# Two-layer hybrid trunk on one core: mixers reworked, three buffers for RWKV's Gram matrices, one for its loaded projections

## Chip, cores and metric

One core of one Trainium2 chip runs the whole program in one launch. The metric is the device time of an execution in microseconds (us), lower is better. PE is the tensor engine (matrix products), DVE the vector engine, ACT the scalar engine, POOL the general-purpose engine, SP the engine whose queue issues most of the DMA transfers.

## What is computed

A trunk of two layers over 1024 prompt tokens and 32 sample tokens (8 sequences of 4), width 1024. Each layer projects its input, runs three groups of heads side by side, projects back, normalises, and runs a gated feed-forward part with a short convolution.

```python
for l in range(DEPTH):                                   # 2
    p = x @ w_in[l]                                      # 1024 -> 1440 | 976 | 1280 columns
    y_a, ... = _rwkv7_mix(p_rw, ...)                     # 6 heads, state 64x64 each
    y_b, ... = _gla_mix(p_gl, ...)                       # 5 heads, chunks of 64
    y_c, ... = _ret_mix(p_rt, ...)                       # 5 heads, rotary, fixed decay
    x = _layer_norm(ALPHA * x + concat([y_a, y_b, y_c]) @ w_out[l])
    f = conv_ffn(x)                                      # gelu(a) * b, 2816 wide, conv of 3 taps
    x = _layer_norm(ALPHA * x + f)

def step(s, inp):                                        # RWKV-7, per token
    r_t, w_t, a_t, b_t, k_t, v_t = inp
    sa = einsum('bhvk,bhk->bhv', s, a_t)
    s = s * w_t + sa[..., None] * b_t + v_t[..., None] * k_t
    return s, einsum('bhvk,bhk->bhv', s, r_t)

def _rms_heads(o):                                       # GLA and retention, per head
    return o * lax.rsqrt(jnp.mean(jnp.square(o), -1) + 1e-6)
```

Outputs are the two token streams and all new states.

## The kernel before

**Tiling.** Tokens are columns in three blocks of 384, 384 and 288 (the last holds the 32 samples first). Channels are rows in tiles of 128. The large products take each operand in two parts (a rounded high part and the rest, made by `split`, L186: ACT copies, POOL or DVE subtracts), and three products per tile and k (`mm3`, L251). The smaller products are plain fp32: each shows as two matmul instructions, a transpose as one.

**Order.** `Tensor` (L101) pins the order of PE's instructions to the order in which the program emits them, and keeps an estimated clock. Work is written as streams that yield either a wait in us, mostly out of the table `AFTER` (L36), or an event of another stream. `run` (L142) emits the first stream that is ready by the estimate, and a filler stream where none is. `post` (L133) puts off a DMA issue in the same way. So PE's order is fixed before the launch: if an operand comes later than the table says, PE stands there, and all behind it.

**Layer, in order.**

1. `group_a(0)` (L431): RWKV's twelve column tiles over block 0, one after the other (`gemm_steps`, L270). Weights come piece by piece through `Feed` (L203): four pieces of split weights at a time, two pieces to a column tile. In layer 0 the input itself is loaded and split here (L291); in layer 1 it comes channel tile by channel tile out of the LayerNorm of layer 0 (`normed`, L1474).
2. RWKV with filler (L909). Four streams over nine batches of 128 tokens (the ninth is the samples): `fronts` loads the projections (tile `x`, XB buffers) and makes the operands `ra` and `bk` (L473); `grams` makes the products within a chunk (`gps` in PSUM, masked by DVE into `gm`, GB buffers, L537) and starts the triangular solve; `toks` makes token-major operands (L563); `chains` joins the solution (`rwkv_merge`, L647) and runs the two chunks that carry the state (`rwkv_core`, L678). The solve (L621) goes to DRAM and back, spread over 96 partitions, with 62 dependent small DVE operations, then by DMA back into `gm`; its buffers `N` and `U` are single. Waits between batches: front i needs `tok` of i-1 and `chained` of i-3; gram i needs `chained` of i-GB, GB = 2; tok i needs `done` of i-2 (L793 to L815). PSUM for all of these is `pm`, two banks. The filler is `group_a` of blocks 1 and 2 and then `group_b` (L847), the token-major columns of GLA and retention (`gt`).
3. GLA, retention, the output projection and its LayerNorm (L1346): nine token tiles each through `gla_front`, `gla_back`, `ret_front`, `ret_back`; `finish` (L979) is the RMS norm and gate at the end of each of the 18. Its inverse root is `rsqrt` (L238): twelve DVE operations on [128, 5]. `yrows` transposes the rows back, `out_proj` (L1315) projects a block and sums for the LayerNorm; `stats` (L945) multiplies the sums with a matrix of ones (`lnm`, `lnv`), ACT takes Ln and Exp; `steps` (L959) applies it channel tile by channel tile: subtract (DVE), multiply (DVE), scale (ACT), split (ACT, POOL).
4. The feed-forward part (L1358 on): up-projection (`pu`), convolution on DVE, gate, down-projection (`pd`). Its first tiles use block 0, then 1, then 2 (`up_blocks`, L1426). PSUM: `pg` three banks, `pd` five.

Of the kernel before, what the change touches and what calls it, by code (L numbers as in the profile page):

```python
# [34 lines left out]
# expected times (us) from a step to what it makes ready  # L35
AFTER = {"key": 5.93, "sh": 3.5, "rkv": 2.0, "block": 6.0, "blockin": 2.5, "x": 3.0, "operands": 8.0, "gram": 0.9, "tv": 0.9, "tb": 0.9, "solve": 24.0, "ud": 4.5, "joined": 4.0, "mask": 1.5, "gd": 4.5, "x11": 1.28, "x21": 1.4, "x22": 0.6, "z": 1.4, "s": 1.58, "am": 2.0, "sx": 1.0, "sout": 3.0, "y": 7.3, "gate": 1.4, "state": 2.5, "done": 7.0, "turn": 2.5, "tokin": 3.36, "ev": 2.25, "gexp": 2.6, "gqt": 1.6, "rrot": 5.5, "rqt": 2.0, "at": 2.5, "qm": 0.8, "vx": 0.9, "gstate": 1.2, "tk": 4.5, "gateout": 4.0, "yin": 2.2, "yout": 4.5, "gnext": 1.2, "rout": 8, "rnext": 0.8, "yt": 0.5, "yready": 1.79, "ln": 3.0, "lnk": 1.5, "lns": 3.0, "ln1": 3.0, "ln2": 9.0}  # L36
# [18 lines left out]
# constant columns  # L55
# [10 lines left out]
class Event:  # L66
    """A time on the tensor engine from which something it has to wait for is expected."""
# [7 lines left out]
class Stream:  # L75
    """Work on the tensor engine in bursts: yields the time (us) until the next one can start, or an Event or a condition."""
# [24 lines left out]
class Tensor:  # L101
    """The tensor engine, its instructions kept in the order of the program, with an estimate of its time (us)."""

    def __init__(self, tc, engine):
        self.tc, self.engine, self.t, self.last, self.posts = tc, engine, 0.0, None, []
        Event.clock = self.clock
# [4 lines left out]
    def order(self, ins, cols, passes):  # L111
        ins = ins.ins
# [20 lines left out]
    def post(self, after, do):  # L133
        """Calls `do` when the time has come: a store that would hold up its queue before."""
# [7 lines left out]
    def run(self, streams, filler):  # L142
        """Emits the streams, the first ready one first, and the filler where none is; ends with the streams."""
# [14 lines left out]
def step_kernel(ctx: ExitStack, tc: tile.TileContext, xT, wA, wB, wO, wU, wD, pp, pb, lora, bg, bgk, shT, cvT, srw, sgl, srt,  # L158
# [27 lines left out]
    def split(dst_h, dst_l, src, le=None):  # L186
        """The two parts of src; returns the instructions."""
        return A.copy(dst_h, src), (le or G).tensor_tensor(dst_l, src, dst_h.bitcast(F32), ALU.subtract)  # L188
# [14 lines left out]
    class Feed:  # L203
        """Weights in two parts, piece after piece ([P, k, c] each), as far ahead as there is room."""
# [28 lines left out]
        def k(self, first, k):  # L233
            """The parts of row k of the matrix whose first piece is `first`, and whether its piece ends with it."""
# [3 lines left out]
    def rsqrt(pl, x, mul, add):  # L238
        """1 / sqrt(x * mul + add), by Newton's steps from the exponent's half."""
# [16 lines left out]
    def xtiles(what, n):  # L256
        """The two parts of a block; before the high part of the third one there is room for the low parts of its samples."""
# [4 lines left out]
    def gemm_ch(w, xs, n, name):  # L262
        """One M-tile of channel-major output over block n."""
        ps = pg.tile([P, 512], F32, tag="g", name=name)[:, :NB[n][1]]
# [1411 lines left out]
```

## Time and profile before

| | |
|---|---|
| device time, median of 3 runs | 3442.24 us (3440.7 to 3452.11) |
| span of the profiled execution | 3430.9 us |
| instructions in it | 59397 |
| PE / DVE / ACT / POOL busy | 3198.4 / 2068.6 / 1434.7 / 1332.6 us |
| layer 0: block 0's projection | 0 to 94 us, PE busy 84.87 |
| layer 0: end of `out_proj` to the first columns of `pu` | 921 to 945 us, PE busy 17.54 |
| layer 1: end of layer 0 to the end of block 0's projection | 1694 to 1840 us, PE busy 122.32 |
| layer 1: GLA, retention, output | 2285 to 2616 us, PE busy 288.35 |
| layer 1: its feed-forward part | 2640 to 3385 us, PE busy 743.88 |

The span is the profiler's, from the first to the last instruction of the program; the device time of the profiled execution itself is not given, and the median of the runs is 11.3 us above the span. A row of a table of groups gives line, engine, operation, names written and read, tile and shapes, count, busy time in us, mean ns of one, then idle time ahead of them and what ended it. A row of the timeline gives start, length, engine, line, names, count, and in brackets the engine's idle time ahead of it and what ended it. A row of the stages gives length, busy time of PE, of its weight loads (PEld), of DVE, ACT and POOL, the granted share of PE's clock, the DMA share and GB/s. Busy time of matrix products is stretched where the clock was granted by half.

### The profile page before, as it was taken

How to read it: one execution, taken by the hardware profiler on the slowest of the kernel's cores; microseconds unless marked ns; L12 is line 12 of the kernel's file. 1: busy time of each engine (PE TensorE's matmuls, PEld its weight loads, DVE VectorE, ACT ScalarE, POOL GpSimd, SP SyncE). 2: the span in 40 equal slices, each digit the busy share in tenths (PEclk: the TensorE clock that was granted, in tenths of full speed). 3: DMA queues.
4: the chain of work that ended last, by engine and by line, in shares of the span. 5: the costliest groups of instructions: out<-in, count | busy, mean ns of one | idle time of the engine just before them, and what ended most of it. 6: DMA issues, size and time to landing. Idle time of an engine off the chain costs nothing.

```text
span 3430.9 us, 59397 instructions
## 1 busy us (share of the span) xinstructions
PE 3198.4 (93%) x22110; PEld 2975.9 (87%) x22110; DVE 2068.6 (60%) x5037; ACT 1434.7 (42%) x3208; POOL 1332.6 (39%) x1660
## 2 busy tenths in 40 slices
PE   9889999988899999999888999999788999999995
PEld 8778888776799999999877888887777999999995
DVE  3577565776756544454746866646777564545457
ACT  6554332334543334333575543323346423333335
POOL 5443222224553334333565522221336433433345
PEclk9789999998999999999998999999989999999998
DMA  7333213433311111111154432234433111111111
GB/s 249 112 110 99 79 54 102 139 115 102 106 60 47 44 44 50 50 44 50 56 164 140 133 91 68 63 128 119 129 94 100 48 44 44 56 44 44 44 44 56
DMA packets 233261, 288.24 MB, mean 84 GB/s; under 512 B 65212, under 2 KB 146908, under 8 KB 232972
## 3 DMA queue, kind: packets, MB, share of 16 engines
q1 hardware_dynamic: 223852, 271.98, 26.3%
q10 hardware_dynamic: 9120, 12.47, 1.2%
q8 instruction: 173, 2.83, 0.4%
q14 instruction: 116, 0.95, 0.1%
HBM read 225.94 MB, written 58.43 MB: 83 GB/s over the span
## 4 chain that ended last, share of the span: by engine, by line
PE 70%; DVE 16%; DMA 4%; ACT 4%; issue 3%; POOL 2%; SPq 1%; ACTq 0%; DVEq 0%; POOLq 0%
PE pu L128 27%; PE pd L128 13%; PE gt L128 9%; PE pa L128 5%; PE po L128 3%; DVE tm L630 2%; DVE U L632 2%; PE zy L128 2%; PE gps L128 2%; PE rop L128 1%; DVE c L1401 1%; PE gop L128 1%; POOL wil L188 1%; DMA N<-gd 1%; DVE s L940 1%
## 5 line engine op out<-in xcount | busy, mean ns | idle before, releaser
L1401 DVE SCALAR_TENSOR_TENSOR c<-u,ppt,c 128x32 f32<-128x32 f32 (+1 forms) x704 | 395.8, 589 | 545.5 <-ACT c L1392 523.8
L188 POOL TENSOR_TENSOR wil<-wir,wih 128x512 fp32r<-128x512 f32 (+1 forms) x264 | 366.3, 1395 | 365.8 <-ACT wih L188 361.2
L128 PE MATMUL gt<-wih,xh 128*128 128x320 f32 (+1 forms) x1008 | 340.1, 339 | 0.9 <-DVE mx L388 0.9
L1448 DVE TENSOR_TENSOR acc<-acc,pd 128x384 f32<-128x384 f32 (+1 forms) x480 | 247.7, 518 | 139.5 <-PE pd L128 137.5
L128 PE MATMUL gt<-wil,xh 128*128 128x320 f32 (+1 forms) x1008 | 316.1, 315 | 6.5 <-POOL wil L188 5.2
L128 PE MATMUL gt<-wih,xl 128*128 128x320 f32 x896 | 281.6, 314 | 0.0
L188 ACT CAST wih<-wir 128x512 fp32r<-128x512 f32 (+1 forms) x296 | 185.6, 637 | 162.4 <-PE po L128 71.5
L128 PE MATMUL pa<-xh,wih 128*128 128x384 f32 (+1 forms) x576 | 216.5, 376 | 20.4 <-DVE mx L388 11.8
L630 DVE TENSOR_TENSOR tm<-U,N 96x60 f32<-96x60 f32 (+24 forms) x558 | 179.1, 321 | 69.9 <-DMA N<-gd 48.4
L128 PEld LDWEIGHTS gt<-wih,xh 128*128 128x128 f32 (+1 forms) x1008 | 187.5, 186 | 38.6 <-issue 21.9
L128 PE MATMUL pa<-xl,wih 128*128 128x384 f32 (+1 forms) x576 | 201.4, 350 | 3.3 <-POOL xl L188 3.0
L128 PE MATMUL pa<-xh,wil 128*128 128x384 f32 (+1 forms) x576 | 200.7, 348 | 3.6 <-POOL wil L188 2.2
L128 PEld LDWEIGHTS gt<-wil,xh 128*128 128x128 f32 (+1 forms) x1008 | 188.5, 187 | 10.2 <-POOL wil L188 9.1
L188 POOL TENSOR_TENSOR hl<-c,hh 128x384 fp32r<-128x384 f32 x132 | 128.1, 971 | 159.6 <-ACT hh L188 133.0
L632 DVE TENSOR_TENSOR U<-U,tm 96x60 f32<-96x60 f32 (+24 forms) x558 | 170.3, 305 | 14.0
L128 PEld LDWEIGHTS gt<-wih,xl 128*128 128x128 f32 x896 | 173.1, 193 | 0.0
L1392 ACT ACTIVATE c<-pu,ppt 128x384 f32<-128x384 f32 (+1 forms) x264 | 172.8, 655 | 0.0
L1380 ACT COPY u<-pu 128x384 f32<-128x384 f32 x176 | 84.1, 478 | 195.2 <-PE pu L128 195.1
L188 ACT CAST hh<-c 128x384 fp32r<-128x384 f32 x132 | 64.4, 488 | 222.4 <-DVE c L1407 222.3
L128 PEld LDWEIGHTS pa<-xh,wih 128*128 128x128 f32 x576 | 119.7, 208 | 35.1 <-DVE mx L388 13.2
L128 PE MATMUL po<-yh,wih 128*128 128x384 f32 (+1 forms) x384 | 138.9, 362 | 9.1 <-DVE ac L1325 6.7
L128 PE MATMUL po<-yh,wil 128*128 128x384 f32 (+1 forms) x384 | 131.7, 343 | 3.7 <-DVE wil L188 3.7
(810 smaller groups left out, 9862.6 us busy)
## 6 DMA issues: line engine op xcount, KB each, us to landing
wir<-in_wA_dram SPq DMA_DIRECT2D x144, 256.0 KB
wir<-in_wO_dram SPq DMA_DIRECT2D x96, 256.0 KB
wir<-in_wB_dram SPq DMA_DIRECT2D x56, 320.0 KB
tokd<-ev SPq DMA_DIRECT2D x112, 160.0 KB
x<-rkvd SPq DMA_DIRECT2D x16, 576.0 KB
tk<-tokd SPq DMA_DIRECT2D x16, 480.0 KB
rkvd<-mx SPq DMA_DIRECT2D x36, 192.0 KB
tk<-tokd SPq DMA_DIRECT2D x16, 400.0 KB
```

Of the source, the lines that this page charges most:

```text
L128: self.order(self.engine.matmul(out, lhsT, rhs, start=start, stop=stop), cols, 4 if rhs.dtype == F32 else 1)
L188: return A.copy(dst_h, src), (le or G).tensor_tensor(dst_l, src, dst_h.bitcast(F32), ALU.subtract)
L630: V.tensor_tensor(tm, U[:, 0:nr, i:i + 1].to_broadcast([4 * ns, nr, 31 - i]), N[:, i:i + 1, i + 1:32].to_broadcast([4 * ns, nr, 31 - i]), ...
L632: V.tensor_tensor(U[:, 0:nr, i + 1:32], U[:, 0:nr, i + 1:32], tm, ALU.add)
L940: self.ends["V"] = V.tensor_tensor(self.s1, acc[0] if k == 1 else self.s1, acc[k], ALU.add)
L1380: A.copy(u[:, 2:386], ps)
L1392: A.activation(c[:, :W], ps, AF.Identity, scale=pc(PP_CV + 4 * t + 2), bias=pc(PP_CV + 4 * t + 3))
L1401: V.scalar_tensor_tensor(cv, src, pc(PP_CV + 4 * t + tap), cv, ALU.mult, ALU.add)
L1448: V.tensor_tensor(acc[n][m], acc[n][m], ps, ALU.add)
```

## The change

- **Pairs of row halves.** Products over 64 rows are emitted alternately for rows 0 to 63 and 64 to 127, each half into its own PSUM bank: `zw`/`za` in `rwkv_front`, the two heads of a pair in `rwkv_gram` (now eight products at a time and one yield of 2 x 0.9 us where there were two of 0.9), and the heads of `ret_front`, whose k no longer carries zeros in the other head's rows (one copy of four columns in place of a copy and two scalings).
- **Transposes.** `tv` and the samples' `tb` in `rwkv_tok` use the transpose instruction, not a product with the identity.
- **Buffers.** GB from 2 to 3, XB from 2 to 1.
- **Table.** Grams of the first two batches wait 5.5 us longer; `x11` goes from 1.28 to 3.0 us.
- **Two column tiles at once.** The first two column tiles of `group_a(0)` run k by k together (`gemm_two`).
- **LayerNorm.** In `steps`, where parts are asked for, multiplication and the split's subtraction alternate between DVE and POOL by channel tile. The statistics' products of block 2 are held back (`Tensor.hold`) and put behind the first two `pu` tiles over block 0; those two take their banks from `pd`.
- **`finish`.** The inverse root is Ln and Exp on ACT, with the table set that has both named ahead of them, in place of `rsqrt`.

```diff
-AFTER = {..., "x11": 1.28, ...}
+AFTER = {..., "early": 5.5, ..., "x11": 3.0, ...}
-GB = 2
-BK, XB = 1, 2
+GB = 3
+BK, XB = 1, 1
...
+    def hold(self, do):
+        self.held = []
+        do()
+        held, self.held = self.held, None
+        return lambda: [self.order(*h) for h in held]
...
+    def gemm_two(feed, first, xs, n, names):
+        ps = [pg.tile([P, 512], F32, tag="g", name=name)[:, :NB[n][1]] for name in names]
+        xh, xl, _ = xs[n]
+        for k in range(KD):
+            for i, p in enumerate(ps):
+                h, lo, _ = feed.k(first + 2 * i, k)
+                mm3(p, h, lo, xh[:, k], xl[:, k], k == 0, k == KD - 1)
+            for _ in range({3: 1, 7: 3}.get(k, 0)):
+                feed.free()
+            if k < KD - 1:
+                yield 0
+        return ps
...
         def group_a(n):
-                ps = yield from gemm_steps(feed, 2 * (n * NA + q), xs, n, f"pa{m}_{n}", True)
+                if n == q == 0:
+                    two = yield from gemm_two(feed, 0, xs, n, [f"pa{i}_{n}" for i in MS[:2]])
+                if two:
+                    ps = two.pop(0)
+                else:
+                    ps = yield from gemm_steps(feed, 2 * (n * NA + q), xs, n, f"pa{m}_{n}", True)
...
         def rwkv_front(s):
-            for i, z in enumerate((zw, za)):
-                for j in range(NPAIR):
+            for j in range(NPAIR):
+                for i, z in enumerate((zw, za)):
...
-            yield AFTER["operands"]
+            yield AFTER["operands"] + (AFTER["early"] if s.b < 2 else 0)
...
         def rwkv_gram(s):
                 for j0, j1 in ((0, 2), (2, 3)):
+                    gps = [pmt("gps")... for _ in range(2)]
+                    for j in range(j0, j1):
+                        for c in range(2):
+                            for h in range(2):
+                                hs = slice(h * 64, h * 64 + 64)
+                                TE.matmul(gps[h][:, j - j0, c], bk(j, c)[hs], ra(j, c)[hs], start=True, stop=True)
                     for h in range(2):
-                        hs = slice(h * 64, h * 64 + 64)
-                        gps = pmt("gps")...
-                        for j in range(j0, j1):
-                            for c in range(2):
-                                TE.matmul(gps[:, j - j0, c], bk(j, c)[hs], ra(j, c)[hs], start=True, stop=True)
-                        V.tensor_tensor(g5[:, j0:j1, :, h], gps, ...)
-                        yield AFTER["gram"]
+                        V.tensor_tensor(g5[:, j0:j1, :, h], gps[h], ...)
+                    yield 2 * AFTER["gram"]
...
         def rwkv_tok(s):
-                TE.matmul(tv[:W, j * P:(j + 1) * P], s.v[:, j], ident, start=True, stop=True)
+                TE.transpose(tv[:W, j * P:(j + 1) * P], s.v[:, j], ident)
...
         class LayerNorm, steps:
-                    (V if hl or k % 2 else G).tensor_tensor(a, a, s2, ALU.mult)
+                    ((G if k % 2 else V) if hl else (V if k % 2 else G)).tensor_tensor(a, a, s2, ALU.mult)
...
-                        for ins, e in zip(split(hl[0][:, k], hl[1][:, k], a), "AG"):
+                        for ins, e in zip(split(hl[0][:, k], hl[1][:, k], a, V if k % 2 else G), "AV" if k % 2 else "AG"):
...
         def finish(op, rows, dst, gate, nw):
-            A.activation(sq, dst, AF.Square)
+            first = A.activation(sq, dst, AF.Square)
...
-            sm = rsqrt(gp_, sm, 1.0 / 64, 1e-6)
+            ins = TE.after(A.preload_act_table_set("natural_log_exp_and_others"), first)
+            TE.after(A.activation(sm, sm, AF.Ln, scale=1.0 / 64, bias=eps(1, rows)), ins)
+            A.activation(sm, sm, AF.Exp, scale=-0.5)
...
         def ret_front(s, tt):
-            A.copy(qT[:, 0:2], tp[:, 0:2 * rows].rearrange("p (g t) -> p g t", g=2))
-            for h in range(2):
-                A.activation(qT[:, 2 + h:6:2], tp[:, 2 * rows:4 * rows]..., AF.Copy, scale=C("h2")[:, h:h + 1])
+            A.copy(qT[:, 0:4], tp[:, 0:4 * rows].rearrange("p (g t) -> p g t", g=4))
...
+            sp = [front("rsp")[:rows, 0:(3 - i) * rows].rearrange("p (h t) -> p h t", t=rows) for i in range(2)]
             for h in range(4):
-                TE.matmul(sp[:rows, h * rows:(h + 1) * rows], qT[:, 2 + h], qT[:, h // 2], start=True, stop=True)
-            s4 = front("rs4")[:rows, 0:rows]
-            TE.matmul(s4, qT[:64, 7], qT[:64, 6], start=True, stop=True)
+                hs = slice((h % 2) * 64, (h % 2) * 64 + 64)
+                TE.matmul(sp[h % 2][:, h // 2], qT[hs, 2 + h // 2], qT[hs, h // 2], start=True, stop=True)
+            TE.matmul(sp[0][:, 2], qT[:64, 7], qT[:64, 6], start=True, stop=True)
...
         def out_proj(n):
-            yield AFTER["ln"]
-            ln.stats()
+            yield AFTER["ln"] if n < 2 else 0
+            if n < 2:
+                ln.stats()
+            else:
+                stats3.append(TE.hold(ln.stats))
...
         def up_conv(t, i, n, w, prev):
-            ps = gemm_ch(w, x1, n, f"pu{t}")
+            ps = gemm_ch(w, x1, n, f"pu{t}", None if t % NJ or n else pd.tile([P, 512], F32, tag="d", name="pu"))
...
         def up_blocks(j, between):
                 hs.append(up_gate(cs, n))
+                if n == 0 and j == 0:
+                    stats3[0]()
```

More of the change, by code (lines that the diff above doesn't have):

```diff
@@ L34 @@
 GW = 320
-AFTER = {"key": 5.93, "sh": 3.5, "rkv": 2.0, "block": 6.0, "blockin": 2.5, "x": 3.0, "operands": 8.0, "gram": 0.9, "tv": 0.9, "tb": 0.9, "solve": 24.0, "ud": 4.5, "joined": 4.0, "mask": 1.5, "gd": 4.5, "x11": 1.28, "x21": 1.4, "x22": 0.6, "z": 1.4, "s": 1.58, "am": 2.0, "sx": 1.0, "sout": 3.0, "y": 7.3, "gate": 1.4, "state": 2.5, "done": 7.0, "turn": 2.5, "tokin": 3.36, "ev": 2.25, "gexp": 2.6, "gqt": 1.6, "rrot": 5.5, "rqt": 2.0, "at": 2.5, "qm": 0.8, "vx": 0.9, "gstate": 1.2, "tk": 4.5, "gateout": 4.0, "yin": 2.2, "yout": 4.5, "gnext": 1.2, "rout": 8, "rnext": 0.8, "yt": 0.5, "yready": 1.79, "ln": 3.0, "lnk": 1.5, "lns": 3.0, "ln1": 3.0, "ln2": 9.0}
+AFTER = {"key": 5.93, "sh": 3.5, "rkv": 2.0, "block": 6.0, "blockin": 2.5, "x": 3.0, "operands": 8.0, "early": 5.5, "gram": 0.9, "tv": 0.9, "tb": 0.9, "solve": 24.0, "ud": 4.5, "joined": 4.0, "mask": 1.5, "gd": 4.5, "x11": 3.0, "x21": 1.4, "x22": 0.6, "z": 1.4, "s": 1.58, "am": 2.0, "sx": 1.0, "sout": 3.0, "y": 7.3, "gate": 1.4, "state": 2.5, "done": 7.0, "turn": 2.5, "tokin": 3.36, "ev": 2.25, "gexp": 2.6, "gqt": 1.6, "rrot": 5.5, "rqt": 2.0, "at": 2.5, "qm": 0.8, "vx": 0.9, "gstate": 1.2, "tk": 4.5, "gateout": 4.0, "yin": 2.2, "yout": 4.5, "gnext": 1.2, "rout": 8, "rnext": 0.8, "yt": 0.5, "yready": 1.79, "ln": 3.0, "lnk": 1.5, "lns": 3.0, "ln1": 3.0, "ln2": 9.0}
 FB, BB = 2, 3
-GB = 2
-BK, XB = 1, 2
+GB = 3
+BK, XB = 1, 1
 WBUFS, RAW = 4, 4
@@ L104, in __init__ @@
     def __init__(self, tc, engine):
-        self.tc, self.engine, self.t, self.last, self.posts = tc, engine, 0.0, None, []
+        self.tc, self.engine, self.t, self.last, self.posts, self.held = tc, engine, 0.0, None, [], None
         Event.clock = self.clock
@@ L111, in order @@
     def order(self, ins, cols, passes):
+        if self.held is not None:
+            self.held.append((ins, cols, passes))
+            return
         ins = ins.ins
@@ L542, in rwkv_gram @@
             if s.smp:
-                for h in range(2):
-                    hs = slice(h * 64, h * 64 + 64)
-                    gps = pmt("gps")
-                    for j in range(NPAIR):
-                        TE.matmul(gps[:64, j * 64:(j + 1) * 64], bk(j)[hs], ra(j)[hs], start=True, stop=True)
-                    V.tensor_tensor(s.gm[:64, :, h * 64:(h + 1) * 64], gps[:64, 0:192].rearrange("p (j t) -> p j t", j=NPAIR),
+                gps = [pmt("gps") for _ in range(2)]
+                for j in range(NPAIR):
+                    for h in range(2):
+                        hs = slice(h * 64, h * 64 + 64)
+                        TE.matmul(gps[h][:64, j * 64:(j + 1) * 64], bk(j)[hs], ra(j)[hs], start=True, stop=True)
+                for h in range(2):
+                    V.tensor_tensor(s.gm[:64, :, h * 64:(h + 1) * 64], gps[h][:64, 0:192].rearrange("p (j t) -> p j t", j=NPAIR),
                                     C("rkmask_s", 64).unsqueeze(1).to_broadcast([64, NPAIR, 64]), ALU.mult)
@@ L581, in rwkv_tok @@
                 for j in range(NPAIR):
[L582 removed]
+                    TE.transpose(tb[:64, j * P:(j + 1) * P], bk(j), ident)
                 A.copy(s.bkt[:64, :, 0:P], tb[:64, 0:384].rearrange("p (j t) -> p j t", j=NPAIR))
@@ L1152, in ret_front @@
             mk = C("smask" if smp else "retmask", rows)
[L1153 removed]
+            sp = [front("rsp")[:rows, 0:(3 - i) * rows].rearrange("p (h t) -> p h t", t=rows) for i in range(2)]
             for h in range(4):
[L1155 to L1160 removed]
+                hs = slice((h % 2) * 64, (h % 2) * 64 + 64)
+                TE.matmul(sp[h % 2][:, h // 2], qT[hs, 2 + h // 2], qT[hs, h // 2], start=True, stop=True)
+            TE.matmul(sp[0][:, 2], qT[:64, 7], qT[:64, 6], start=True, stop=True)
+            for i in range(2):
+                V.tensor_tensor(at[:, i:5:2], sp[i], mk.unsqueeze(1).to_broadcast([rows, 3 - i, rows]), ALU.mult)
         def ret_back(s, tt, dst):
```

20 lines of the change are left out of this document (8 added, 12 removed).

## The prediction

> **What bounds the kernel now.** The page comes first, then the busy times by stage, the waits, the groups of matrix products, and last the timeline around the places that the change touches.
>
> ```profile
> span 3430.9 us, 59397 instructions
> PE 3198.4 (93%) x22110; PEld 2975.9 (87%) x22110; DVE 2068.6 (60%) x5037; ACT 1434.7 (42%) x3208; POOL 1332.6 (39%) x1660
> ```
>
> ```profile
> 94.00:592.00 498.00, 461.70 (x3656) 404.18 (x3657) 319.82 (x1105) 202.82 (x465) 165.53 (x174) 0.90 0.32 90
> 592.00:921.00 329.00, 288.86 (x2189) 245.50 (x2188) 234.81 (x558) 133.54 (x349) 112.73 (x94) 0.93 0.40 122
> 945.00:1694.00 749.00, 746.04 (x4652) 743.22 (x4651) 404.37 (x711) 276.23 (x587) 308.98 (x472) 1.00 0.16 49
> 1840.00:2285.00 445.00, 417.26 (x3508) 364.35 (x3507) 301.42 (x1067) 185.27 (x425) 150.09 (x158) 0.94 0.33 91
> ```
>
> PE bounds it. The feed-forward stage (945 to 1694) is full at full clock, and nothing there changes. The RWKV stages (94 to 592, 1840 to 2285) are 93% busy, but at a granted clock of 0.90 and 0.94: 0.10 x 498 + 0.06 x 445 = 77 us of clock are lost there beside 64 us of idle time. There is filler in these stages, so PE work, idle time and lost clock taken out of them all shorten the whole, if the streams can go faster too. The third kind of stage (592 to 921) has 40 us of idle PE, with DVE at 71%.
>
> ```profile
> PE lnm L128 <- DVE s L940: 23.4, 5, 6.7
> PE tps L128 <- ACT x L656: 16.3, 6, 4.9
> PE gps L128 <- DVE bk L533: 12.5, 5, 6.0
> PE ytp L131 <- DVE yt L990: 20.2, 10, 4.0
> ```
>
> These are waits of PE: total, times, longest. All four are places of the change.
>
> **PE work removed.**
>
> ```profile
> L128 PE MATMUL gps<-ra,bk 64*128 64x128 f32 x384 | 69.8, 323 | 15.2 <-DVE bk L533 12.5 <-DVE gm L559 2.7
> L128 PE MATMUL rsp<-rqT 128*128 128x128 f32 x128 | 19.4, 299 | 0.0
> L128 PE MATMUL tv<-cs,v 128*128 128x128 f32 x96 | 17.2, 327 | 0.0
> L131 PE MATMUL tb<-cs,bk 128*128 128x128 f32 x96 | 16.9, 287 | 0.0
> L128 PE MATMUL zy<-sav,gm 128*64 128x64 f32 x384 | 27.6, 222 | 0.0
> L128 PE MATMUL up<-sav,bkt 128*64 128x64 f32 x384 | 18.2, 230 | 2.4 <-ACT sav L693 2.4
> ```
>
> ```profile
> 372.65 0.60 PE L128 MATMUL zw<-sh,lorat 64*128 64x128 f32 x3
> ...
> 373.31 0.27 PE L128 MATMUL za<-sh,lorat 64*128 64x128 f32 x1
> 373.31 0.27 PE L128 MATMUL zw<-sh,lorat 64*128 64x128 f32 x1
> 373.42 0.49 PE L128 MATMUL za<-sh,lorat 64*128 64x128 f32 x3
> ```
>
> Products on different row halves do overlap: `zw` (rows 0 to 63) and `za` (64 to 127), written one after the other, start in the same 10 ns, a pair every 0.11 us, which is what one costs alone. `gps` never gets that, because filler stands between its halves. Alternated, its 69.8 us become 34.9 at best. The nearest row for alternating halves of the other kind, `up` against `zy` of the same shape, gives 18.2 / 27.6 = 0.66, so 46: saved between 24 and 35, none if the pairs don't form. I take **27**. `rsp` is 128 rows with zeros in half of them; by the same halving 19.4 loses up to 9.7: **7**. `tv` makes 48 products of 96 instructions, `tb` 96 transposes of 96 (176 ns each), so `tv` falls to 8.4: **8**. `zw`/`za` overlap in part already: 12 instructions from 372.65 to 373.91, 1.26 us, against 6 x 0.11 + 0.27 = 0.93; 0.33 x 16 batches: **5**.
>
> **Waits and clock in the RWKV stages.** `early` and `x11` put filler where PE stood: of 12.5 + 16.3 us I take **23** (filler exists to the end of both stages; if it didn't, nothing). The clock:
>
> ```profile
> 99.40:112.40 13.00, 13.00 (x43) 10.79 (x43) 2.25 (x4) 2.04 (x5) 4.28 (x5) 0.50 0.43 122
> 117.00:125.00 8.00, 8.00 (x50) 7.40 (x49) 5.01 (x7) 5.28 (x11) 4.16 (x4) 1.00 0.42 132
> ```
>
> After the 6 us stand before the first Gram products, PE is busy 13.00 of 13.00 us and still runs at 0.50 while half-row products alternate with filler; full clock comes back only behind them. The Trainium skill, "TensorE: Matmul & The Clock Gate", Part 1, has full clock return after about 3.4 us of sustained work; this trace disagrees, and the measurement decides. By that rule the stand would cost some 2 us of clock.
>
> By the rows it costs 0.5 x 13 us and more. Without the stand, and with both halves of the array at work, most such episodes should go: of the 77 us I take **20** (0 to 45).
>
> So PE frees 27 + 8 + 5 + 23 + 20 = 83 us in the two RWKV stages. **Can the streams follow?** That is the third Gram buffer's part.
>
> ```profile
> 282.62 0.60 PE L128 MATMUL zw<-sh,lorat 64*128 64x128 f32 x3
> 313.79 0.86 PE L128 MATMUL zy<-sav,gm 128*64 128x64 f32 x12
> 314.58 1.16 PE L128 MATMUL gps<-ra,bk 64*128 64x128 f32 x8
> 411.98 1.16 PE L128 MATMUL gps<-ra,bk 64*128 64x128 f32 x8
> 82.74 0.60 PE L128 MATMUL zw<-sh,lorat 64*128 64x128 f32 x3
> 99.37 2.07 PE L128 MATMUL gps<-ra,bk 64*128 64x128 f32 x8 [6.01 <-DVE bk L533]
> ```
>
> Batch 4's `gps` (314.58) starts 0.8 us behind batch 2's last `zy`: it waited for `gm`. Its operands start at 282.62, and from there to ready took 99.37 - 82.74 = 16.6 us in batch 0, so it could go at 299.2, 15 us sooner; batch 6 (372.65, 411.98) 23 us sooner. Its solve starts as much sooner, and the chain that waits for it. Three even batches a layer at 19 us are 57 us; the odd ones gain nothing directly, since their front waits for `tok` and that for `done` of i-3. I take three quarters: 43 us a layer, 86 in all. Engine and streams agree, and the smaller counts: **83**. XB = 1 costs nothing: the next front comes behind `tok`, long after the last read of `x`; if that cover went, one load of some 4 us a batch would show. The samples' `am` and `sx` use `x` for one pair only, one after the other.
>
> **Output LayerNorm to feed-forward.**
>
> ```profile
> 927.46 1.33 PE L128 MATMUL lnm<-s,cs 128*128 128x288 f32 x2 [6.57 <-DVE s L940]
> 939.82 4.82 POOL L188 TENSOR_TENSOR x1l<-ac,x1h 128x288 fp32r<-128x288 f32 x6 [0.46 <-ACT x1h L188]
> 1002.28 46.05 PE pu L128 x288
> ```
>
> The two held products let 48 `pu` products (48 x 46.05 / 288 = 7.7 us) run where PE stands 6.57 us. Late next is block 2: it is wanted after 96 products, 15.4 us from 921, so about 937 to 939; today its last low part ends at 944.6 with POOL alone, and POOL and DVE in turn save perhaps 3. I count a new wait of 3 us: (6.6 - 3) x 2 = **7** (-5 to 20, the latter with the half clock there). `pu`'s first two banks come from `pd`, free then.
>
> **Starts.**
>
> ```profile
> 10.93 1.98 ACT L188 CAST wih<-wir 128x512 fp32r<-128x512 f32 x3 [0.19 <-DMA wir<-in_wA_dram]
> 11.62 4.04 POOL L188 TENSOR_TENSOR wil<-wir,wih 128x512 fp32r<-128x512 f32 x3 [1.56 <-ACT wih L188]
> 14.85 0.33 PE L128 MATMUL pa<-xh,wil 128*128 128x384 f32 x1
> ```
>
> In layer 0 `gemm_two` puts the second tile's weights, split at 10.93 to 12.9, ahead of the first tile's k = 1, where today the first tile is nearly done at 14.85. That speaks against the change: up to 8 us later; weights that arrive in the meantime give most back: **2** lost (0 to 9).
>
> ```profile
> 1705.21 0.45 PE L128 MATMUL pa<-xh,wih 128*128 128x384 f32 x1 [0.32 <-ACT xh L188]
> 1724.52 0.34 PE L128 MATMUL pa<-xh,wil 128*128 128x384 f32 x1
> ```
>
> In layer 1 the first two tiles take 19.6 us for 48 products (7.7 at full pace), the first waiting for every channel tile. Both at once fill these waits: **6** gained (0 to 8).
>
> **`finish`.**
>
> ```profile
> L247 DVE SCALAR_TENSOR_TENSOR nw<-nw,nw 128x5 f32<-128x5 f32 (+3 forms) x162 | 39.0, 241 | 3.1
> L956 ACT ACT_TABLE_LOAD x12 | 15.4, 1283 | 0.2
> L1027 ACT ACTIVATE eb<-bp 128x2 f32<-128x2 f32 (+1 forms) x18 | 3.4, 188 | 0.0
> ```
>
> Twelve DVE steps near 240 ns are 2.9 us in a row; now two ACT steps near 190 ns behind a table load of 1.28 us, partly under the reduction: about 1.5. DVE loses 36 x 2.9 = 104 us of work, of which little was last. ACT gains at most 36 x 2 x 1.28 = 92 us, with gates' tanh loading the other set back. I take **5** gained, out of the 20.2 us that PE waits for `yt` (25 gained to 10 lost). The Trainium skill, "ScalarE: Activation LUTs", section "What ACT_TABLE_LOAD costs", speaks against this edit: about 2.66 us for a switch with its drain. By it the gain would be near none; the rows show 1283 ns and the next ACT step right behind.
>
> **Sum.** 83 + 7 (`rsp`) + 7 - 2 + 6 + 5 = 106. Against the profiled span: 3430.9 - 106 = 3325; with the 11.3 us by which the median of the runs, 3442.2, lies above the span, **3336 us**.
>
> **Rivals.** (1) *The streams don't shorten*: solves, one buffer each for their input and output, stay the pace; saved PE time goes into filler that is done earlier, and the last stage waits as before. Then 7 + 7 - 2 + 6 + 5 and about 10 of the RWKV part remain: 33 us, 3409. For it: the odd batches. (2) *Pairs don't form, or the clock stays low*: 27, 7 and 20 go, 52 remain, 3390. The Trainium skill, "TensorEngine Tiling (Array Packing)", Key Properties, says that a change of tiling mode drains the engine. The `gps` rows already are in half-row mode, and the change halves the number of turns between them and filler. (3) *The streams shorten fully*: 57 us a layer (31 more in all), clock loss down by 45 (25 more): 162 gained, 3280. (4) *Slower: solves hold SP's queue.* `post` issues a solve's DMA back 24 us after the solve is written; with three Gram buffers every solve lies beside a chain on DVE, takes longer, and SP, in order, waits with weights, stores and front loads behind it. It decides once a solve exceeds 24 us by more than the four pieces of weights cover, about 8 us of filler. At 12 us for each of 16 batches: 192 - 106 = 86 lost, 3528. Against it: PE waits little for weights today. Of a change that doesn't do what it says only (1) is left, in the third buffer.
>
> **How the numbers follow.** Forecast 0.47, (1) 0.20, (2) 0.12, (3) 0.15, (4) 0.06. Measurement of this kernel can tell 0.3%, 10 us, from no change. All but (4) are faster, but the low end of (1) touches no change: faster 0.91, same 0.03, slower 0.06. The range takes in (3) and, above, the bad ends of (1): 3275 to 3425.
>
> **What would show it.** `gps` busy near 40 us and its two halves starting together; clock above 0.95 in the RWKV stages; waits for `bk` and `x11` gone; even batches' `gps` no longer right behind a `zy`; no wait before the third `lnm`, a small one before block 2's `pu`; `nw` in `finish` gone. It is wrong if the RWKV stages keep their length, or if PE's waits move to weights.

## The result, and the profile after

The changed kernel takes 3391.66 us in the median of 4 runs (3373.66 to 3398.29), the kernel before 3441.47 beside it: a ratio of 0.985, with a 95% interval of 0.9814 to 0.9886. That is 50 us faster where 106 were forecast. Measured again beside the experiments it gave 3390.5 and 0.9868 (0.9848 to 0.9889).

The page of the changed kernel:

```profile
span 3396.5 us, 58910 instructions
...
PE 3158.1 (93%) x22050; PEld 2927.8 (86%) x22050; DVE 2002.9 (59%) x4605; ACT 1501.7 (44%) x3294; POOL 1335.3 (39%) x1660
```

The span is 34 us shorter. (The 11 us that the prediction laid around the span were none: these runs last 1.8 us longer than their span, so the profiled execution of before was one of the faster ones.) PE is busy 40 us less and idle no less. To see where, the mixers are cut in four stretches, the same places in each kernel: from a layer's first `zw` to the end of RWKV, and from there to the first `pu`. Length, then busy us and instructions of PE, PEld, DVE, ACT and POOL, then PE's granted clock. First the kernel before, then the changed one:

```profile
83.00:591.00 508.00, 471.02 (x3712) 412.74 (x3712) 322.43 (x1113) 212.77 (x487) 169.04 (x177) 0.90 0.32 92
591.00:929.00 338.00, 291.39 (x2199) 247.67 (x2198) 241.97 (x566) 135.81 (x354) 117.45 (x97) 0.92 0.40 122
1798.00:2284.00 486.00, 454.97 (x3725) 399.25 (x3724) 321.84 (x1118) 211.95 (x489) 172.59 (x180) 0.94 0.36 100
2284.00:2624.00 340.00, 290.79 (x2205) 247.34 (x2205) 239.96 (x565) 134.73 (x354) 116.37 (x97) 0.92 0.40 121
sum 1672.00, PE 1508.17 PEld 1307.00 DVE 1126.20 ACT 695.26 POOL 575.45; mean PE 377.04 PEld 326.75 DVE 281.55 ACT 173.81 POOL 143.86
```

```profile
82.00:549.00 467.00, 418.03 (x3591) 365.43 (x3589) 319.18 (x1114) 213.29 (x483) 159.35 (x172) 0.93 0.34 96
549.00:894.00 345.00, 311.88 (x2287) 260.75 (x2286) 196.75 (x342) 171.95 (x399) 118.93 (x101) 0.90 0.40 122
1766.00:2243.00 477.00, 431.80 (x3594) 375.30 (x3592) 327.00 (x1115) 205.79 (x480) 163.45 (x176) 0.91 0.35 97
2243.00:2585.00 342.00, 309.38 (x2306) 260.04 (x2306) 194.01 (x342) 171.12 (x400) 119.79 (x99) 0.92 0.40 123
sum 1631.00, PE 1471.09 PEld 1261.51 DVE 1036.93 ACT 762.16 POOL 561.52; mean PE 367.77 PEld 315.38 DVE 259.23 ACT 190.54 POOL 140.38
```

Idle PE in the two RWKV stretches is 37 + 31 = 68 us before and 49 + 45 = 94 after: it grew by 26 where the forecast took 23 away. Behind RWKV it fell from 47 + 49 = 96 to 33 + 33 = 66, where 5 were forecast for `finish` and 7, net, for the held statistics. The clock of the profiled execution did not rise. Half the time that the records show at 0.50 is counted as clock lost; length less idle less lost clock is called PE's work. In the four stretches, taken from instruction to instruction and not in whole us as above, work fell by 48, the 47 of the prediction; idle by 4; lost clock grew by 9. The two feed-forward stages grew by 7.8 and 4.4 us (block 3's statistics lie in them now), and layer 1's start got 4.4 shorter.

The waits of PE over the whole program, changed kernel: total, times, longest. In such a wait PE and all that is behind it in its order stand, so it is called a stand below.

```profile
PE lnm L138 <- DVE s L971: 15.6, 5, 6.8
PE up L138 <- ACT sav L724: 15.4, 5, 7.2
PE ups L138 <- ACT x L692: 13.9, 5, 3.7
...
PE gps L138 <- DVE gm L590: 7.5, 3, 4.4
PE xps L138 <- DMA gm<-ud: 7.4, 3, 5.0
PE gps L138 <- DVE bk L562: 6.7, 5, 3.4
...
PE ytp L141 <- DVE yt L1024: 3.8, 2, 2.9
```

The 16.3 us at `tps` are gone. One and two steps further down the same chain, at `ups` and `up`, stand 29.3 us (`up` had 2.4, `ups` 0.8). The 20.2 us at `ytp` are 3.8. The Gram products by form, and on the timeline where they follow a filler:

```profile
L138 PE MATMUL gps<-ra,bk 64*128 64x128 f32 x384 | 34.5, 305 | 13.9 <-DVE gm L590 7.5 <-DVE bk L562 6.2
```

```profile
103.69 1.16 PE L138 MATMUL gps<-ra,bk 64*128 64x128 f32 x16
```

The pairs form: 16 instructions in the 1.16 us that 8 took. 69.8 us became 34.5.

What holds the copies of the chain is seen on ACT, before the longest stand at `up` (328.44 to PE, 7.15 us):

```profile
316.63 0.48 ACT L719 COPY zs<-zy 64x384 f32<-64x384 f32 x1 [0.55 <-PE zy L138]
325.48 0.52 ACT L549 ACTIVATE pi<-L 128x384 f32<-128x384 f32 x1 [8.37 <-DVE L L548]
325.91 0.51 ACT L551 ACTIVATE pt<-L 128x384 f32<-128x384 f32 x1
326.44 0.43 ACT L907 COPY ev<-gt 128x320 f32<-128x320 f32 x1
326.76 1.26 ACT L554 ACTIVATE kf<-ta,dv 128x128 f32<-128x128 f32 x3
327.93 0.46 ACT L724 COPY sav<-sp 64x384 f32<-64x384 f32 x1
```

On ACT nothing passes `pi`, which belongs to a later batch's front and waits 8.37 us for a scan on DVE that lies among a solve's steps. `sav`, which the chain needs and whose product was done near 319, comes behind it. In all ten stands at `ups` and `up` the copy starts 1.8 to 8.6 us after its product's end, with other work of ACT in between: in two of them (7.2 and 5.8 us) that is a front's `pi`, in the other eight it is copies and small steps of other streams, most of which had themselves waited for DVE or POOL.

### The profile page after: what moved, and what is told of

It reads as the page before. It is cut to its first block, busy times and chain, and to the rows that moved or that the text cites. A ratio compares the mean times of both kernels' runs of the same rounds, so it can differ in the third digit from the quotient of the medians.

```text
span 3396.5 us, 58910 instructions
## 1 busy us (share of the span) xinstructions
PE 3158.1 (93%) x22050; PEld 2927.8 (86%) x22050; DVE 2002.9 (59%) x4605; ACT 1501.7 (44%) x3294; POOL 1335.3 (39%) x1660
## 5 line engine op out<-in xcount | busy, mean ns | idle before, releaser
L138 PE MATMUL gt<-wil,xh 128*128 128x320 f32 (+1 forms) x1008 | 322.9, 322 | 8.9 <-POOL wil L198 8.4
L138 PE MATMUL pa<-xh,wih 128*128 128x384 f32 (+1 forms) x576 | 206.2, 358 | 23.9 <-ACT wih L198 10.4
L138 PEld LDWEIGHTS gt<-wil,xh 128*128 128x128 f32 (+1 forms) x1008 | 193.6, 192 | 14.9 <-POOL wil L198 13.1
L138 PE MATMUL pa<-xl,wih 128*128 128x384 f32 (+1 forms) x576 | 194.2, 337 | 1.2 <-POOL xl L198 0.7
L663 DVE TENSOR_TENSOR U<-U,tm 96x60 f32<-96x60 f32 (+24 forms) x558 | 176.0, 315 | 13.7
```

The lines of the kernel that those rows point to most:

```text
L138: self.order(self.engine.matmul(out, lhsT, rhs, start=start, stop=stop), cols, 4 if rhs.dtype == F32 else 1)
L663: V.tensor_tensor(U[:, 0:nr, i + 1:32], U[:, 0:nr, i + 1:32], tm, ALU.add)
```

## The experiments

All were timed in the same way, kernels of a group on one chip beside the kernel before (3432 to 3440 us there). Idle is PE's in the four stretches of the one profiled execution (length less busy, from instruction to instruction, so that a sum over whole us can differ by 1). Lost clock is each run's span times (1 - its granted clock), in the median of a kernel's runs: 175 us for the kernel before (59 runs beside all groups, 158 to 193).

| kernel | what | us | ratio (95%) | idle, RWKV / all four | lost clock |
|---|---|---|---|---|---|
| before | | 3436 | 1 | 68 / 164 | 175 |
| changed (c1) | | 3390.5 | 0.9868 (.9848-.9889) | 92 / 159 | 156 |
| e1 | changed, two Gram buffers | 3381.4 | 0.9839 (.9811-.9867) | 81 / 150 | 157 |
| e6 | changed, solve in pieces | 3396.8 | 0.9870 (.9844-.9895) | 99 / 166 | 156 |
| e3 | changed, Newton in `finish` | 3416.8 | 0.9946 (.9929-.9963) | 90 / 172 | 171 |
| e4 | changed, statistics not held | 3395.5 | 0.9882 (.9863-.9901) | 89 / 172 | 166 |
| e2 | changed, early 0, x11 1.28 | 3364.2 | 0.9793 (.9774-.9813) | 82 / 140 | 153 |
| e9 | changed, early 0, x11 3.0 | 3371.5 | 0.9818 (.9795-.9841) | 91 / 147 | 155 |
| e10 | changed, early 5.5, x11 1.28 | 3358.9 | 0.9779 (.9758-.9800) | 89 / 144 | 134 |
| e16 | changed, early 5.5, x11 0.6 | 3346.6 | 0.9739 (.9714-.9763) | 83 / 137 | 137 |
| e17 | changed, early 5.5, x11 2.1 | 3384.0 | 0.9845 (.9818-.9873) | 92 / 152 | 169 |
| e11 | e2 with two Gram buffers | 3388.5 | 0.9867 (.9846-.9887) | 93 / 153 | 154 |
| e12 | e2, pairs counted once | 3362.2 | 0.9782 (.9755-.9810) | 85 / 143 | 148 |
| e13 | e10, longer pause in `gram` | 3380.0 | 0.9833 (.9813-.9854) | 89 / 149 | 162 |
| e7 | before, new products alone | 3405.1 | 0.9909 (.9885-.9933) | 97 / 190 | 170 |
| e14 | before, Gram pairs alone | 3416.0 | 0.9930 (.9913-.9947) | 87 / 177 | 171 |
| e15 | before, the other products | 3453.4 | 1.0047 (1.0030-1.0064) | 91 / 187 | 199 |
| e8 | before, buffers alone | 3457.4 | 1.0058 (1.0039-1.0077) | 74 / 172 | 194 |

The theory at first, P: the gain is the 48 us of products that PE no longer has; stands taken away come back elsewhere. Its rivals: B, the prediction's, that the third Gram buffer lets the streams follow; and H, that this buffer is what puts a solve beside the next front and so makes the new stands. In every run on the buffers GB and XB change together; XB was not run alone, but no PE wait in the changed kernel's trace is for a load of `x`.

**e1, two buffers**, in the changed kernel:

```
-GB = 3
-BK, XB = 1, 1
+GB = 2
+BK, XB = 1, 2
```

> The changed kernel with two Gram buffers and two of the loaded projections, as before. Theory P (what the change gained is the 48 us of product time that it took from PE; all else nets to nothing): same as the changed kernel, 3382 to 3402 us. Theory B (the prediction's: the third buffer lets the streams follow, and without it PE's saved time is stood away): 3415 us or more, even batches' gps right behind a zy again. Theory H (the third buffer lays a solve on DVE beside the next front, ACT stands at pi for L, and the chain's copies behind it are late): faster than the changed kernel, 3370 to 3382 us, with PE's waits for sav at L724 (7.2 and 5.8 us) gone.

The waits at the two steps, and those that took their place, e1:

```profile
PE gps L138 <- DVE gm L590: 12.1, 6, 4.4
PE rsp L138 <- ACT qT L1077: 11.7, 4, 5.6
...
PE gp L138 <- ACT gm L697: 9.0, 5, 2.5
PE ups L138 <- ACT x L692: 7.1, 3, 4.0
...
PE up L138 <- ACT sav L724: 4.7, 5, 2.3
```

H is right on the long stands for `sav`: none is over 2.3 us, and the 29.3 us of both steps are 11.8. The time, 3381.4 us, lies at the upper end of H's range, but 0.9839 isn't to be told apart from 0.9868 (c1) and 0.985, so the stands that went are not shown to be worth anything. B, by which the kernel would be slower without the buffer, falls for this table of times.

**e8, buffers alone**: `GB` 3 for 2 and `XB` 1 for 2 in the kernel before.

> The kernel before with three Gram buffers and one of the loaded projections, nothing else. Theory P: within 10 us of 3441. Theory B: the RWKV stages end up to 43 us sooner each, but PE's work is the same, so only idle time and lost clock can go: 3400 to 3425 us. Theory H: stands of PE for sav and x appear, 3445 to 3465 us.

20 us slower. The same four stretches:

```profile
82.00:565.00 483.00, 447.85 (x3558) 389.09 (x3559) 319.59 (x1114) 206.94 (x476) 159.58 (x171) 0.90 0.33 92
565.00:928.00 363.00, 318.08 (x2354) 270.98 (x2353) 240.03 (x567) 140.41 (x364) 122.21 (x104) 0.91 0.40 120
1797.00:2268.00 471.00, 432.46 (x3553) 376.12 (x3551) 312.37 (x1115) 205.64 (x477) 164.69 (x175) 0.93 0.35 98
2268.00:2644.00 376.00, 322.14 (x2381) 276.44 (x2380) 240.24 (x567) 141.12 (x365) 122.17 (x103) 0.92 0.38 116
```

RWKV does end sooner, by 25 and 15 us, so the buffer shortens the streams; but the stretches behind grow by 25 and 36. PE has the same work: filler that was done under RWKV is now done behind it, and 40 us of shorter streams are worth nothing here. B's price of 43 us a layer falls, and so does P's "within 10 us": lost clock rose by 19 (194 against 175). H's range holds the time, but not its waits: `up` stands 1.0 us for `sav`, `ups` 2.7.

**e6, the solve in pieces.**

```
+                for a in range(0, 31, 4):
+                    TE.post(0.75 * a, lambda a=a: steps(a, min(31, a + 4)))
-                for i in range(31):
+                def steps(a, z):
+                  for i in range(a, z):
```

> The changed kernel with the solve's 31 steps written in eight pieces, 3 us of PE time apart, so that a front's steps on DVE can stand between them. Theory H: ACT's wait of 8.4 us at pi for L goes, and with it PE's long waits for sav and x; idle PE in the two RWKV stages falls from 49 and 45 us to 30 to 35 each and some half-clock time goes with it: 3355 to 3380 us. Rival (PE's waits come from the order and the table, not from DVE's queue; or the solve itself becomes late): within 6 us of the changed kernel's 3392, or slower, with waits for ud or gm in place of those for sav.

No change. On ACT, at the same place as above:

```profile
317.46 0.48 ACT L723 COPY zs<-zy 64x384 f32<-64x384 f32 x1
326.06 0.52 ACT L549 ACTIVATE pi<-L 128x384 f32<-128x384 f32 x1 [8.13 <-DVE L L548]
```

DVE's order did not change with the order in which the steps are written: the scan still lies behind the same step of the solve. So this run tells nothing on H; that the solve on DVE causes the longest stands is read from timelines and not shown by an experiment.

**e7, products alone.** `zw` with `za`, `gps`, `tv`, `tb` and the retention's scores as in the change; all else as before.

> The kernel before with the new products alone: zw/za and gps written pair by pair, tv and the samples' tb as transposes, the retention's products on half the rows. Theory P: 48 us of PE work go and nothing else, 3393 us (3383 to 3403). Theory B: with two Gram buffers the streams don't follow, so most of it turns into waits: 3415 to 3430 us. Prediction's rival of a clock that stays low: PE work falls by 48 but lost clock rises by 20 or more, 3413 us.

31 us faster: between P and B. Work in the four stretches falls by 53, but idle in RWKV grows from 68 to 97. PE's waits there, e7:

```profile
PE gps L128 <- DVE gm L561: 13.1, 11, 4.3
PE tps L128 <- ACT x L658: 12.7, 3, 4.9
...
PE gp L128 <- ACT gm L668: 8.8, 5, 5.7
PE bp L128 <- ACT bkt L593: 6.5, 3, 3.4
```

Before the change `gps` waited 2.7 us for `gm`. The pairs take both banks of that pool at once, so the second group of products finds neither read yet. (This is the reading of the rows; a pool with more banks was not run.)

**c1, the yardstick; e2, the old table:**

```
-"early": 5.5 ... "x11": 3.0
+"early": 0.0 ... "x11": 1.28
```

> The changed kernel as it is, as the yardstick for the runs beside it: 0.985 of the kernel before, about 3388 us (3375 to 3400).

> The changed kernel with the two old times of the table (early 0, x11 1.28). The prediction's term (filler put where PE stood takes 23 us of waits away, and clock with them): slower than the changed kernel by 20 to 40 us, the waits for bk and for x11 back at 12 and 16 us. Theory P (a stand that is taken away there comes back at the next place where the order and the other engines differ): within 8 us of it, idle PE in the RWKV stages as much as in the changed kernel (49 and 45 us) under other names.

e2 is 26 us faster than the changed kernel, outside every range. It isn't that the two new times bring nothing: they cost. The stands that they were to fill are back, e2:

```profile
PE gps L138 <- DVE bk L562: 20.8, 8, 6.0
...
PE tps L138 <- ACT x L687: 6.4, 4, 2.1
```

and still idle is 140 against 159; the three stands of the chain, `tps`, `ups` and `up`, sum to 13.1 us in e2 and 29.3 in the changed kernel.

**e3, `finish`:**

```
-            ins = TE.after(A.preload_act_table_set("natural_log_exp_and_others"), first)
-            TE.after(A.activation(sm, sm, AF.Ln, scale=1.0 / 64, bias=eps(1, rows)), ins)
-            A.activation(sm, sm, AF.Exp, scale=-0.5)
+            sm = rsqrt(gp_, sm, 1.0 / 64, 1e-6)
```

> The changed kernel with the twelve small DVE steps back in finish in place of the two on ACT. If the 30 us of idle PE that the stretches between RWKV and the feed-forward lost come from this edit: idle there rises from 33 and 33 us to 45 or more each, 10 to 25 us slower. If they come from the split of LayerNorm's channels between DVE and POOL and the held statistics: within 5 us of the changed kernel.

26 us slower, 1 us beyond the range. The wait that the edit was aimed at carries it, e3:

```profile
PE ytp L141 <- DVE yt L1022: 34.5, 9, 8.6
```

against 3.8 in the changed kernel. Idle behind RWKV is 82 against 67 us (39 and 43, short of the 45 each that were expected), and lost clock 171 against 156.

**e4, statistics not held** (the first `pu` keeps its bank of `pd`):

```
-            yield AFTER["ln"] if n < 2 else 0
-            if n < 2:
-                ln.stats()
-            else:
-                stats3.append(TE.hold(ln.stats))
+            yield AFTER["ln"]
+            ln.stats()
```

> The changed kernel with the third block's statistics where they were, ahead of the first up-projection. The prediction's term (7 us for two layers): 5 to 10 us slower, PE's wait before the third lnm back at about 6.6 us a layer, and the 7.8 and 4.4 us by which the feed-forward stages grew gone. Rival (block 2 is late anyway, and PE stands there instead): within 3 us.

5 us slower, with intervals that overlap. Its trace has the wait back, e4:

```profile
904.70 1.33 PE L138 MATMUL lnm<-s,cs 128*128 128x288 f32 x2 [6.61 <-DVE s L971]
```

and idle behind RWKV at 83 instead of 67, but its feed-forward stages are 8.3 and 7.7 us shorter than those of c1. Most of what is gained ahead of the first `pu` is given back behind it.

**e9 and e10, one time each.** A new pair of theories, X (x11 does the harm) and E (early does it), with S (chance of how the streams fall) beside them.

> The changed kernel with early at 0 and x11 left at 3.0. Putting both times back made the changed kernel 26 us faster (3364 against 3390.5), against the prediction. Theory X (x11 does the harm: the chain's steps come 1.7 us later in every batch and its copies for x and sav on ACT then stand behind a front's): no faster than the changed kernel, 3383 to 3397 us, PE's waits for sav L724 and x L692 at 6 us or more in layer 0. Theory E (early does it: two batches a layer start their Gram products 5.5 us later, and every later batch with them): 3360 to 3375 us. Theory S (order alone: any shift of the streams against each other moves the time by 10 us or so): between.

> The changed kernel with x11 at 1.28 and early left at 5.5. Theory X: 3360 to 3375 us, PE's waits for sav L724 and x L692 small. Theory E: 3383 to 3397 us. Theory S: between.

`early` alone is harmless (0.9779 against 0.9793). x11 alone costs 7 us, with intervals that overlap; x11 on top of `early` costs 32. X holds for e10, which rules out E; but e9, at 3371.5, lies in the range that E gave it, which rules out X by itself. So neither time alone does the harm. In e9 `tps`, `ups` and `up` stand 5.3 us together: 29.3 us there are seen only with both new times (e2, with neither, has 5.0 us for `sav`).

**e16 and e17, the curve.** `"x11"` at 0.6 and at 2.1, `early` at 5.5.

> The changed kernel with x11 at 0.6 (early left at 5.5). If the pause itself costs (31 us between 1.28 and 3.0, or 18 us a microsecond): some 10 us faster than with 1.28, 3343 to 3355 us. If PE's stand at tps, which it would meet sooner, costs as much as the pause: 3355 to 3375 us, with waits at tps of 10 us or more. If it is chance how the streams fall: anywhere from 3355 to 3395 us.

> The changed kernel with x11 at 2.1 (early left at 5.5). If the pause itself costs: between 3359 and 3390, about 3374 us (3368 to 3381). If it is chance how the streams fall: outside of that.

0.6, 1.28, 2.1 and 3.0 give 3346.6, 3358.9, 3384.0 and 3390.5 us, and idle of 137, 144, 152 and 159: the longer the pause, the slower. The intervals of the first two and of the last two overlap; the step from 1.28 to 2.1 is clear. (e17 lies 3 us above its range, which the expectation counted for chance; its runs spread over 16 us.) From end to end it is 44 us for 2.4 us of pause; 16 batches times 2.4 are 38. About half of the 44 is idle time (22) and the other half lost clock (137 against 156). The sum row and the merge's stands of e16:

```profile
sum 1579.00, PE 1442.25 PEld 1241.16 DVE 1030.03 ACT 761.92 POOL 559.73; mean PE 360.56 PEld 310.29 DVE 257.51 ACT 190.48 POOL 139.93
```

```profile
PE tps L138 <- ACT x L687: 6.8, 5, 2.5
PE up L138 <- ACT sav L724: 4.3, 1, 4.3
...
PE ups L138 <- ACT x L692: 1.3, 1, 1.3
```

With almost no pause PE stands 12.4 us at the three steps together; with 3.0 it stands 29.3, and the chain is later besides. e16 is the fastest version of all.

**e11, the old table with two buffers.** Both edits, of e1 and e2.

> The changed kernel with the old table and with two Gram buffers and two of the loaded projections. If the third buffer harms (alone, on the kernel before, it cost 20 us; taken from the changed kernel it gave some 9): faster than with the old table alone, 3340 to 3358 us. If it harms only with the new table: within 8 us of 3364. If the streams need it: slower, 3375 us or more.

24 us slower than e2, so with the old table the third buffer (with XB at 1) is worth 24 us; with the new one nothing that can be told (e1), on the kernel before -20 (e8). Its value isn't its own.

**e12, the order's own clock.** In `Tensor.order`, `self.t += max(0.025, cols * passes / 2400) / self.share`, with a share of 2 at `zw`, `za` and `gps`.

> The changed kernel with the old table, and the order's own clock counting a pair of products on different halves of the rows (zw with za, the two gps) as one: so far it counts both in full, runs ahead by about 2 us a batch, and takes the streams' next steps too early. If that is where the products' saving of 48 us lost 17: idle PE in the RWKV stages falls by 10 to 20 us in all, 3344 to 3356 us. If not: within 8 us of 3364.

No difference; the miscounted pairs are not where the products' saving went.

**e13, a longer pause between the Gram products**, in e10:

```
-                    yield 2 * AFTER["gram"]
+                    yield 4 * AFTER["gram"]
```

> The version with x11 at 1.28 and early at 5.5 (3359 us), with 3.6 us instead of 1.8 of other work behind each pair of Gram products. If the stands before the second pair (gps for gm, 15 us in the two layers) only need filler: they fall below 5 us, idle PE in all four mixer stretches from 144 to about 134, 5 to 15 us faster. If a stand that is taken away comes back elsewhere, as with x11: idle stays at 140 to 150 or grows, same or slower by up to 25 us.

The stand goes, as asked, from 14.8 us for `gm` to none (3.2 us for other things are left at `gps`), and the time is 21 us longer. Idle is 149 against 144, lost clock 162 against 134, and `up` now stands 9.7 us, e13:

```profile
PE up L138 <- ACT sav L724: 9.7, 5, 3.6
```

It is x11 over again.

**e14 and e15, the products divided.**

> The kernel before with the Gram products alone written pair by pair. Product time falls by about 32 us. Bank theory (both banks are taken at once, so the second pair and what follows stands): idle in the RWKV stages grows from 68 by 15 to 25 us, gain 8 to 17 us: 3417 to 3426. Theory that any shorter product only meets the streams earlier: idle grows in proportion, by some 15 to 18 us of the 27. If pairs are clean here: 3404 or less.

> The kernel before with all the new products but the Gram ones (zw with za, tv and tb as transposes, the retention's halves). Product time falls by about 20 us. Bank theory: idle in the RWKV stages stays near 68, gain 15 to 20 us: 3414 to 3420. The other: idle grows by 9 to 12 us, gain about 10.

The Gram pairs alone give 24 us for about 30 us of work, more than the 8 to 17 of the bank theory. Idle in RWKV is up by 19, within its range and that of the other theory, but only 8 of the 19 are for `gm`. The others alone take as much work away (21 us by their own rows, counted at the clock granted under them) and make the kernel 14 us *slower*, which neither theory allowed, with idle up by 23 and lost clock by 24. -24 and +14 don't make the -31 of both. The bank theory explains its 8 us; the rest of the idle time does not belong to any one product.

## Why the prediction was right or wrong

**PE's products: right.** 47 forecast, 48 less work in the trace. As the rows have it, `gps` gave 35 us (71.2 to 35.7, its few sample products among them), `tv` 9, the retention's scores 9 (20.6, and 9.0 for the fifth head, which has its own tile `rs` before, to 20.1), `zw` and `za` 6 (23.3 to 17.5 together). Part of that is half clock: counted at the clock granted under each row they gave 27, 6, 9 and 6, where 27, 8, 7 and 5 were taken.

**Waits in the RWKV stages: wrong, and this is the step that failed.** The prediction put it so: "`early` and `x11` put filler where PE stood: of 12.5 + 16.3 us I take 23". The filler did go there: the stands at `tps` are gone, those for `bk` fell from 12.5 to 6.7 us. But the pause was priced at nothing. It lies in the chain of each of 16 batches, 1.72 us longer than before: 27.5 us of a stream on which the later batches wait. From a layer's first `zw` to its last `zy`, both layers together, RWKV lasts 877 us with the old times (e2), 885 with the new `early` alone (e10), 899 with the new `x11` alone (e9), and 904 and 913 in the two profiled executions of the changed kernel. The curve from e16 to c1 shows the price in time: shorter pauses are faster from end to end. And the stand moves down the chain (29.3 us at `ups` and `up`), where ACT's copies come behind work of other streams. So instead of 23 gained the two times cost 26 (e2), which is 49 of the 56 us that were missing. The rest is no clean sum: `finish` gave 21 more than forecast, the products' 47 brought 31 (e7), and the parts don't add.

The curve was taken with `early` at 5.5. With `early` at 0 the pause made RWKV 22 us longer as well, but the kernel only 7 us slower, which is not told apart from nothing (e9). Why the time follows in one case and not in the other stays open beyond the stands that only both bring.

**Why idle time grew with fewer products.** e7 shows that it did before any table was touched. The likely reading, argued and not shown: when PE is through sooner, what is behind it in a stream (copies on ACT, masks on DVE) takes as long as before, and PE reaches the next product earlier than its operand. Part of it, 8 to 10 us at `gps`, goes with the two banks that a pair takes at once (e14, e7); for the remainder no single edit was found, and the edits don't add.

**"Can the streams follow?"** On the kernel before, the third buffer shortens RWKV's streams by 25 and 15 us and not by 43 a layer (e8). The claim that engine and streams agree and the smaller counts was too simple: where PE is the bound, shorter streams only move filler, as e8's longer stretches behind show. With the rest of the change and the old table it does more: RWKV, as measured above, lasts 962 us before, 934 in e11 without the buffer and 877 in e2 with it, so 57 us go with the buffer and 85 with all edits, and the time falls by 24 (e2 against e11). That it does so because the products came first is likely but not shown, since e2 and e11 hold the other edits too; with the longer pause its worth can't be told from nothing (e1).

**Clock: right in size over the whole kernel, not shown for its place.** 20 forecast of the RWKV stages; over the runs of the whole kernel 175 us became 156 to 159. The single profiled executions show 165 before and 168 after, and two executions of the same changed kernel differ by 22 (168 and 146) at the same idle time (160 and 159). In the two RWKV stretches the records have 77 us lost before, 75 and 65 in these two. So a single trace can't tell a clock term of 20 us here.

**`finish`: mechanism right, size wrong.** 5 taken, between 25 gained and 10 lost; e3 says 26. The prediction counted a table load of 1.28 us against the 2.9 us of DVE steps and took a quarter of the wait for `yt`; the wait went almost whole. The load's 36 x 1.28 us lie on ACT:

```profile
L1018 ACT ACT_TABLE_LOAD x36 | 46.2, 1283 | 0.6
```

The Trainium skill, "ScalarE: Activation LUTs", "What ACT_TABLE_LOAD costs", gives about 1.28 us for the load, as this row has it, and 2.66 us a switch with a drain, by which the gain would have been near none. The drain isn't seen here: ACT is idle 0.6 us ahead of all 36 loads, and in the whole trace the next ACT step starts 12 ns behind a load in the median. With loads that other steps need again, ACT makes 115 of them where e3 makes 69, 59 us more, and e3 shows the gain all the same.

**LayerNorm to feed-forward: not contradicted**, 7 forecast, 5 measured and not told apart from 0 (e4). **Starts: right**, by the stages alone, since `gemm_two` was not run by itself: layer 0 unchanged (2 lost forecast), layer 1 4.4 us shorter (6).

**The rivals.** The time came out at the second (3390), but by chance and not by it: pairs form, and lost clock fell. Nor was it the first, in which RWKV keeps its length. Solves that hold SP's queue (4) are not seen at that price: PE waits for a DMA only at `xps`, 7.4 us in all, and its waits for split weights rose from 17 to 30 us over the program, 6 of that at the two starts.

## What to carry to other kernels

Before filler is put where the bound engine stands in a stream, multiply the pause by the times the stream runs through it, and ask whether that stream sets an end: the stand is paid where operands happen to be late, the pause, in the worst case seen here (`early` at 5.5), in every round. Shorter instructions on the bound engine are worth less than their time when each is followed by a copy or a mask elsewhere (e7: 53 us of work gave 31). And where streams share in-order queues, test a change's parts together as well as alone: the third buffer was worth -20, about 0 or +24 us by what stood beside it.

## What the runs showed of the hardware

In these records the clock of PE goes with the rows that its products use, and not only with whether it is busy. In the records half-clock stretches are multiples of 3.41 us (3.4, 6.8, 10.2, 13.7). I cut the traces of 19 of these executions, the kernel before among them, in such steps and weighed PE's busy time by the share of the 128 rows in use. After a full-clock step with less than 0.4 the next was at half clock in 531 of 535 cases; with 0.6 and more in 8 of 15,713. A step at half clock with less than 0.7 was followed by a full one in 6 of 701 cases, with 0.9 and more in 553 of 616. Among half-clock steps in which PE was busy all the time (over 0.99), those under 0.7 were followed by full clock in 1 of 182. Small products count too: of such busy half-clock steps with 0.9 and more, all 359 were followed by full clock where less than a fifth of the time went to products of at most 128 columns, but 2 of 22 where more than four fifths did. Under 0.7 and with less than a fifth in small products it was 0 of 81, so the rows matter by themselves. The Trainium skill, "TensorE: Matmul & The Clock Gate", Part 1, has the gate follow how busy PE is over a free-running window of about 3.4 us. The window agrees with these records; that a busy PE on few rows stays at half clock is what they add. It is a count over traces and no experiment, and of two products that overlap only the first was weighed.

The kernel writes the two halves of a pair into a PSUM bank each, which here takes both banks of the pool at once: `gps` stands 13.1 us for `gm` in e7 where 2.7 were. Whether two halves could share a bank was not run.

A solve's small steps on DVE last 0.20 us on their own and 0.76 where POOL is busy for more than half of them (898 and 218 steps of the changed kernel; 0.20 and 0.80 before). The two are seen together; no run moved POOL's work away.
